# Sparse convolution on one core: uncast loads through four half-pair buffers, casts on ScalarE and GpSimd, stores on ScalarE's queue

## The chip, the core and the metric

The kernel runs on one core of a Trainium2 chip. The metric is the device time of one execution in microseconds (us). A profile's span, from the first to the last instruction, is 1.7 to 2.1 us shorter here than the time of the same execution. PE is TensorE, DVE is VectorE, ACT is ScalarE, POOL is GpSimd, SP is SyncE, which here only issues DMAs.

A run counts as fast when it is within 1.5% of the fastest run of the same kernel. Ratios are the mean time of one kernel's fast runs over that of the other's fast runs of the same rounds, so they are not quite the ratios of the medians quoted beside them. The profiled run of the kernel before (132.03 us) bears the state slow in its record, but it lies within the four runs that the first comparison rests on (131.89 to 132.76 us), so its profile stands for them.

## The reference

```python
x:      (16, 64, 64, 64) float32      # batch, channels in, h, w
weight: (128, 64, 3, 3)  float32      # 90% of it zeros
output[b, co] += weight[co, ci, kh, kw] * x_pad[b, ci, kh:kh+h, kw:kw+w]   # pad 1
```

It is a 3x3 convolution with padding. The kernel computes it densely. Two images make a pair: their 2 x 64 input channels fill the 128 partitions. There are eight pairs.

## The kernel before

A pair is worked off in four blocks of 16 rows, and blocks are numbered 0 to 31 through the whole kernel. For a block, GpSimd adds neighbouring rows into `s`, TensorE makes a shared product from `s` (6 matmuls) and two more from `x` (24 matmuls), ScalarE copies the shared product from PSUM to `pc`, and VectorE adds `pc` to the other two and writes the output tile `o`. Block 0 alone is computed directly.

```python
x_pool = tile_pool(name="x", bufs=1)             # eight bf16 tiles, one per pair
o_pool = tile_pool(name="o", bufs=7)
...
nc.sync.dma_start(out=w_sb, in_=weight...)
x_head = const_pool.tile([128, HEAD, W], FP32)   # first 36 rows of pair 0, uncast
for a, b in ((0, 9), (9, HEAD)):
    nc.sync.dma_start(out=x_head[:, a:b, :], in_=pair(0)[:, a:b, :])
nc.gpsimd.dma_start(out=xs[0][:, HEAD:H, :], in_=pair(0)[:, HEAD:H, :])   # fp32 -> bf16 in the DMA
...
for p in range(1, NP):
    nc.gpsimd.dma_start(out=xs[p], in_=pair(p))                           # fp32 -> bf16 in the DMA
...
def twos(p, o, r0):
    s = s_pool.tile([128, 8, W], BF16, name="s")                          # three buffers
    nc.gpsimd.tensor_tensor(out=s, in0=xs[p][:, r0:r0+16:2, :], in1=xs[p][:, r0+1:r0+16:2, :], op=ADD)
    shared = product([(s, G1, 0, 1)], 8)
    ...                                      # pc[n] = scalar.copy(shared[n])
    ...                                      # o[n] rows = even/odd product + pc[n], on VectorE
for p in range(NP):
    for blk in range(4): ...
    if not last:
        for n in range(2):
            nc.sync.dma_start(out=out[2 * p + n], in_=o[n])               # 2 MB each, 16 KB rows
```

The last pair is stored in two halves of 32 rows.

Of the kernel before, what the change touches and what calls it, by code (L numbers as in the profile page):

```python
# [8 lines left out]
FP32 = mybir.dt.float32  # L9
BF16 = mybir.dt.bfloat16  # L10
# [12 lines left out]
G0, G1, G2, G21, G01 = range(5)  # L23
# [4 lines left out]
def kernel(  # L28
# [6 lines left out]
    nc = tc.nc  # L35

    B, C_IN, H, W = x.shape
    C_OUT, _, KH, KW = weight.shape
    assert (B, C_IN, H, W) == (16, 64, 64, 64) and (C_OUT, KH, KW) == (128, 3, 3)
    NP = B // 2  # L40
    HEAD = 36

    const_pool = ctx.enter_context(tc.tile_pool(name="const", bufs=1))
    x_pool = ctx.enter_context(tc.tile_pool(name="x", bufs=1))
    s_pool = ctx.enter_context(tc.tile_pool(name="s", bufs=3))
    p_pool = ctx.enter_context(tc.tile_pool(name="pc", bufs=4))
    o_pool = ctx.enter_context(tc.tile_pool(name="o", bufs=7))
# [7 lines left out]
    def pair(p):  # L55
        return x[2 * p : 2 * p + 2].rearrange("n i h w -> (n i) h w")

    xs = [x_pool.tile([128, H, W], BF16, name=f"x{p}") for p in range(NP)]
    w_sb = const_pool.tile([C_OUT, C_IN * KH * KW], FP32, name="w_sb")
    nc.sync.dma_start(out=w_sb, in_=weight.rearrange("o i kh kw -> o (i kh kw)"))  # L60
    x_head = const_pool.tile([128, HEAD, W], FP32, name="x_head")
    for a, b in ((0, 9), (9, HEAD)):
        nc.sync.dma_start(out=x_head[:, a:b, :], in_=pair(0)[:, a:b, :])  # L63
    nc.gpsimd.dma_start(out=xs[0][:, HEAD:H, :], in_=pair(0)[:, HEAD:H, :])  # L64
    ident = const_pool.tile([128, 128], BF16, name="ident")
    make_identity(nc, ident)
    for p in range(1, NP):
        nc.gpsimd.dma_start(out=xs[p], in_=pair(p))  # L68


    idle_rhs = const_pool.tile([128, 128], BF16, name="idle_rhs")
# [12 lines left out]
    def tap(g, kw, n):  # L84
        return wT[64 * n : 64 * n + 64, g, (kw - n) % 3, :]

    def cast_x(copy, a, b):
        copy(out=xs[0][:, a:b, :], in_=x_head[:, a:b, :])  # L88

    def cast(g, copy, a, b):  # L90
        k = 3 * g + a % 3
        copy(out=w_bf4[:, g, a:b, :], in_=w_v[:, k : k + b - a, :])  # L92

    def transposed(g):
        wps = psum_pool.tile([128, 4, 128], FP32, name="ps")
        for j in range(3):
            src = w_bf[:, g, C_IN * j : C_IN * (j + 2)]
            nc.tensor.matmul(wps[:, j, :], src, ident, start=True, stop=True)  # L98
        return wps[:, 0:3, :]

    def difference(g, wps):
        nc.vector.tensor_tensor(out=wT[:, g], in0=wps, in1=wT[:, G1], op=SUB)  # L102
# [3 lines left out]
    cast(G0, nc.vector.tensor_copy, 0, 3)  # L106
    cast(G0, nc.vector.tensor_copy, 3, 4)
    cast(G2, nc.scalar.copy, 0, 3)
    cast(G2, nc.vector.tensor_copy, 3, 4)
    cast_x(nc.vector.tensor_copy, 0, 9)  # L110
    nc.scalar.copy(out=wT[:, G1], in_=transposed(G1))  # L111
    ps0 = transposed(G0)
    nc.vector.tensor_copy(out=wT[:, G0], in_=ps0)
    ps2 = transposed(G2)
    nc.scalar.copy(out=wT[:, G2], in_=ps2)
    cast_x(nc.scalar.copy, 9, 18)
    difference(G01, ps0)
    difference(G21, ps2)
    cast_x(nc.vector.tensor_copy, 18, HEAD)


    def product(terms, rows):
# [22 lines left out]
    def direct(p, o, r0, rows):  # L145
        ps = product(
            [(xs[p], G1, r0, 1), (xs[p], G0, r0 - 1, 1), (xs[p], G2, r0 + 1, 1)], rows
        )
        nc.scalar.copy(out=o[0][:, r0 : r0 + rows, :], in_=ps[0])  # L149
        nc.vector.tensor_copy(out=o[1][:, r0 : r0 + rows, :], in_=ps[1])  # L150

    def twos(p, o, r0):
        t0 = r0 // 2
        s = s_pool.tile([128, 8, W], BF16, name="s")
        nc.gpsimd.tensor_tensor(  # L155
            out=s, in0=xs[p][:, r0 : r0 + 16 : 2, :], in1=xs[p][:, r0 + 1 : r0 + 16 : 2, :], op=ADD
        )
        shared = product([(s, G1, 0, 1)], 8)
        pc = []
        for n in range(2):  # L160
            c = p_pool.tile([128, 8, W], FP32, name="pc")
            nc.scalar.copy(out=c, in_=shared[n])  # L162
            pc.append(c)
        even = [(xs[p], G21, r0 + 1, 2), (xs[p], G0, r0 - 1, 2)]
        odd = [(xs[p], G01, r0, 2), (xs[p], G2, r0 + 2, 2)]
        for first, terms in ((r0, even), (r0 + 1, odd)):
            ps = product(terms, 8)
            for n in range(2):
                nc.vector.tensor_tensor(  # L169
                    out=o[n][:, first : r0 + 16 : 2, :], in0=ps[n], in1=pc[n], op=ADD  # L170
                )

    for p in range(NP):
        o = [o_pool.tile([C_OUT, H, W], FP32, name="o") for _ in range(2)]
        last = p == NP - 1
        for blk in range(4):
            r0 = 16 * blk
            if BLOCKS[p][blk] == "T":
                twos(p, o, r0)
            else:  # L180
                for r, rows in ((r0, 8), (r0 + 8, 8)):
                    direct(p, o, r, rows)
            if last and blk % 2 == 1:
                for n in range(2):
                    rows = slice(r0 - 16, r0 + 16)
                    nc.sync.dma_start(out=out[2 * p + n][:, rows, :], in_=o[n][:, rows, :])
        if not last:
            for n in range(2):
                nc.sync.dma_start(out=out[2 * p + n], in_=o[n])


# [28 lines left out]
```

## Time and profile before

| kernel before | value |
|---|---|
| median time, 4 runs | 132.28 us (131.89 to 132.76) |
| span of the profiled run | 130.3 us |
| TensorE's first matmul on `x` / last matmul ends | 7.7 / 118.3 us |
| a steady block (30 matmuls) | 3.16 to 3.24 us |
| block 2 / 8 / 17 / 28 starts | 22.1 / 41.3 / 70.0 / 105.3 us |

First the page of the profile: the span in 40 equal slices (busy share of a slice in tenths; 9 is 90% or more), the DMA queues (packets, MB, time of their packets as a share of 16 engines' span), and the chain that ended last.

```profile
PE   6662499999999999999999999999999999993000
...
PEclk9985559999999999999999999999999999999655
DMA  4999999999999999999999999999599929999990
...
q1 hardware_dynamic: 3024, 35.03, 64.6%
q0 software_dynamic: 1152, 7.80, 29.1%
...
PE 79%; DMA 9%; DVE 1%; issue 1%; SPq 1%; ACT 1%; DVEq 0%
```

TensorE is full from the seventh slice (19.5 us) to its end, and it is 79% of the chain. The clock row shows half speed from about 9 to 19 us, around a gap in TensorE's work. The DMA row is full too, but for the slices near 92 and 104 us, where the engines wait for TensorE to finish a pair. So two resources are nearly exhausted at once. The second view cuts the span into stretches: first the length of the stretch, then busy us of PE, PEld (TensorE's loading of weights), DVE, ACT and POOL with instruction counts, the granted clock, DMA share and GB/s written by the DMAs (a casting load counts its bf16 bytes).

```profile
20.00:40.00 20.00, 20.00 (x190) 9.94 (x187) 15.06 (x24) 7.11 (x14) 7.61 (x7) 1.00 1.03 251
...
70.00:80.00 10.00, 10.00 (x96) 5.01 (x94) 7.82 (x14) 3.22 (x6) 3.46 (x3) 1.00 1.01 428
80.00:120.00 40.00, 38.28 (x360) 18.92 (x355) 31.36 (x51) 12.88 (x24) 10.38 (x9) 1.00 0.89 376
```

The 428 GB/s of 70 to 80 us is the pace of uncast stores alone. All 50.6 MB at 430 GB/s are 118 us.

### The profile page before, as it was taken

The numbers are of one execution on the slowest core, as the hardware profiler recorded it, in microseconds if no ns is written. First come the engines' busy times: TensorE is split into PE (matmuls) and PEld (weight loads), VectorE is DVE, ScalarE is ACT, GpSimd is POOL, SyncE is SP. The second block draws the span as 40 slices with busy tenths as digits, with TensorE's granted clock in tenths as the row PEclk, the third lists the DMA queues.
The fourth block names the chain that finished last, engine by engine and source line by source line (L and its number), as shares of the span: only waits on it lengthen the run. The fifth ranks groups of instructions, "written<-read, shape, count | busy, mean of one in ns | idle before, by whom it ended". The sixth has DMA issues, their size and how long they took to land.

```text
span 130.3 us, 2488 instructions
## 1 busy us (share of the span) xinstructions
PE 110.6 (85%) x1002; PEld 56.0 (43%) x1002; DVE 83.0 (64%) x136; ACT 38.0 (29%) x70; POOL 40.7 (31%) x45
## 2 busy tenths in 40 slices
PE   6662499999999999999999999999999999993000
PEld 6430144445444544454445445544544454440000
DVE  0350425778777868787777777777777777777000
ACT  3500313333333333333243333333333333330000
POOL 6900463333333333333333333324333330000000
PEclk9985559999999999999999999999999999999655
DMA  4999999999999999999999999999599929999990
GB/s 136 217 297 228 216 209 226 209 216 216 302 325 307 327 322 314 362 428 438 423 425 428 433 423 433 428 428 443 244 408 403 403 86 402 458 385 415 415 410 18
DMA packets 4188, 42.99 MB, mean 330 GB/s; under 512 B 464, under 2 KB 464, under 8 KB 976
## 3 DMA queue, kind: packets, MB, share of 16 engines
q1 hardware_dynamic: 3024, 35.03, 64.6%
q0 software_dynamic: 1152, 7.80, 29.1%
q8 instruction: 8, 0.13, 0.4%
q14 instruction: 4, 0.03, 0.1%
HBM read 17.07 MB, written 33.55 MB: 389 GB/s over the span
## 4 chain that ended last, share of the span: by engine, by line
PE 79%; DMA 9%; DVE 1%; issue 1%; SPq 1%; ACT 1%; DVEq 0%
PE ps L136 79%; DMA x_head<-in_x_dram 9%; DVE o L169 1%; ACT x L88 1%; DVEq L215 0%; SPq L63 0%; SPq L60 0%; DVEq L169 0%
## 5 line engine op out<-in xcount | busy, mean ns | idle before, releaser
L136 PE MATMUL ps<-x,wT 64*128 64x504 bf16 (+3 forms) x780 | 91.4, 381 | 6.7 <-ACT x L88 4.2
L169 DVE TENSOR_TENSOR o<-ps,pc 128x512 f32<-128x512 f32 x124 | 77.8, 686 | 22.4 <-PE ps L136 20.1
L136 PEld LDWEIGHTS <-wT 64*128 64x128 bf16 x966 | 52.4, 96 | 60.4 <-issue 10.4
L155 POOL TENSOR_TENSOR s<-x 128x512 bf16<-128x512 bf16 x31 | 35.6, 1152 | 65.6 <-PE ps L136 43.4
L162 ACT COPY pc<-ps 128x512 f32<-128x512 f32 x62 | 33.3, 589 | 64.3 <-issue 61.8
L136 PE MATMUL ps<-s,wT 64*128 64x512 bf16 (+1 forms) x186 | 25.8, 380 | 0.0
L88 DVE CAST x<-x_head 128x576 bf16<-128x576 f32 (+1 forms) x2 | 1.2, 611 | 7.5 <-DMA x_head<-in_x_dram 7.5
L75 PE MATMUL ps<-idle_rhs 128*128 128x128 bf16 x27 | 3.1, 313 | 1.0 <-DVE idle_rhs L72 1.0
L68 POOL DMA_DIRECT2D x<-in_x_dram x7 | 3.7, 551 | 0.0
L150 DVE COPY o<-ps 128x512 f32<-128x512 f32 x2 | 1.4, 688 | 3.4 <-PE ps L136 3.4
L75 PEld LDWEIGHTS <-idle_rhs 128*128 128x128 bf16 x27 | 2.8, 149 | 1.0 <-DVE idle_rhs L72 1.0
L88 ACT CAST x<-x_head 128x576 bf16<-128x576 f32 x1 | 0.7, 672 | 8.2 <-DMA x_head<-in_x_dram 8.2
L92 DVE CAST w_bf<-w_sb 128x192 bf16<-128x192 f32 (+1 forms) x4 | 1.2, 360 | 2.5 <-DMA w_sb<-in_weight_dram 2.5
L149 ACT COPY o<-ps 128x512 f32<-128x512 f32 x2 | 1.2, 582 | 3.6 <-PE ps L136 3.6
L92 ACT ACT_TABLE_LOAD x1 | 1.3, 1283 | 0.7 <-PEq L204 0.7
L98 PE MATMUL ps<-ident,w_bf 128*128 128x128 bf16 x9 | 1.2, 308 | 0.0
L92 ACT CAST w_bf<-w_sb 128x64 bf16<-128x64 f32 (+1 forms) x2 | 0.7, 417 | 1.4 <-DMA w_sb<-in_weight_dram 1.4
L102 DVE TENSOR_TENSOR wT<-ps,wT 128x384 bf16<-128x384 f32 x2 | 1.0, 549 | 0.0
L98 PEld LDWEIGHTS <-w_bf 128*128 128x128 bf16 x9 | 0.8, 130 | 0.4 <-DVE w_bf L92 0.4
L64 POOL DMA_DIRECT2D x<-in_x_dram x1 | 0.7, 696 | 0.8 <-POOLq L204 0.8
L72 DVE MEMSET idle_rhs<- 128x64 uint32 x1 | 0.1, 112 | 0.8 <-PEq L204 0.8
L111 ACT CAST wT<-ps 128x384 bf16<-128x384 f32 x1 | 0.5, 478 | 0.4 <-PE ps L98 0.4
(8 smaller groups left out, 1.9 us busy)
## 6 DMA issues: line engine op xcount, KB each, us to landing
out_dram<-o SPq DMA_DIRECT2D x14, 2048.0 KB, 14.4
x<-in_x_dram POOLq DMA_DIRECT2D x7, 1024.0 KB, 26.1
out_dram<-o SPq DMA_DIRECT2D x4, 1024.0 KB, 9.4
x_head<-in_x_dram SPq DMA_DIRECT2D x1, 864.0 KB, 12.3
x<-in_x_dram POOLq DMA_DIRECT2D x1, 448.0 KB, 8.8
w_sb<-in_weight_dram SPq DMA_DIRECT2D x1, 288.0 KB, 2.7
x_head<-in_x_dram SPq DMA_DIRECT2D x1, 288.0 KB, 6.0
```

The costliest lines, as they stand in the source:

```text
L68: nc.gpsimd.dma_start(out=xs[p], in_=pair(p))
L75: nc.tensor.matmul(idle_ps, idle_rhs, idle_rhs, start=True, stop=True)
L88: copy(out=xs[0][:, a:b, :], in_=x_head[:, a:b, :])
L92: copy(out=w_bf4[:, g, a:b, :], in_=w_v[:, k : k + b - a, :])
L98: nc.tensor.matmul(wps[:, j, :], src, ident, start=True, stop=True)
L102: nc.vector.tensor_tensor(out=wT[:, g], in0=wps, in1=wT[:, G1], op=SUB)
L136: nc.tensor.matmul(ps[n][:, lo:hi, c_lo:c_hi], tap(g, kw, n), src[q, a:b:step, c_lo + kw - 1 : c_hi + kw - 1], start=(i == 0), stop=(i == ...
L149: nc.scalar.copy(out=o[0][:, r0 : r0 + rows, :], in_=ps[0])
L150: nc.vector.tensor_copy(out=o[1][:, r0 : r0 + rows, :], in_=ps[1])
L155: nc.gpsimd.tensor_tensor(out=s, in0=xs[p][:, r0 : r0 + 16 : 2, :], in1=xs[p][:, r0 + 1 : r0 + 16 : 2, :], op=ADD)
L162: nc.scalar.copy(out=c, in_=shared[n])
L169: nc.vector.tensor_tensor(out=o[n][:, first : r0 + 16 : 2, :], in0=ps[n], in1=pc[n], op=ADD)
```

## The change

The intent: the loads of pair 0 no longer compete with seven casting loads, TensorE starts sooner, GpSimd generates no DMA work, and idle time of ScalarE and GpSimd is used for the casts. Each half-pair (1 MB, 8 KB per partition) lands as fp32 in one of four buffers `f`. ScalarE casts a pair's first half and GpSimd its second, at places in program order that `CAST_AFTER` lists: after block 1 pair 1, after block 3 pair 2, and so on. Loads would block stores on SP's in-order queue, so stores go to ScalarE's queue, issued a block late. The diff, cut to its core:

```diff
-    x_pool = ctx.enter_context(tc.tile_pool(name="x", bufs=1))
+    f_pool = ctx.enter_context(tc.tile_pool(name="f", bufs=4))
+    x_pool = ctx.enter_context(tc.tile_pool(name="x", bufs=4))
...
-    nc.gpsimd.dma_start(out=xs[0][:, HEAD:H, :], in_=pair(0)[:, HEAD:H, :])
-    for p in range(1, NP):
-        nc.gpsimd.dma_start(out=xs[p], in_=pair(p))
+    halves = []
+    for p in range(NP):
+        for half in range(2):
+            f = f_pool.tile([128, HALF, W], FP32, name="f")
+            cuts = (0, 9, HALF) if not halves else (0, HALF)
+            for a, b in zip(cuts, cuts[1:]):
+                r = HALF * half
+                nc.sync.dma_start(out=f[:, a:b, :], in_=pair(p)[:, r + a : r + b, :])
+            halves.append(f)
...
+    cast_x(nc.gpsimd.tensor_copy, 0, 1)
...
+    CAST_AFTER = {1: 1, 3: 2, 5: 3, 7: 4, 9: 5, 12: 6, 16: 7}
     for p in range(NP):
         for blk in range(4):
             ...                                   # the block, as before
+            store()                               # what was queued, on nc.scalar
+            q = CAST_AFTER.get(4 * p + blk)
+            if q is not None:
+                cast_x(nc.scalar.copy, q, 0)
+                cast_x(nc.gpsimd.tensor_copy, q, 1)
+            if p in (0, NP - 1): ...              # queue stores of halves
+            elif blk == 3:
+                stores += [(out[2 * p + n], o[n]) for n in range(2)]
-        if not last:
-            for n in range(2):
-                nc.sync.dma_start(out=out[2 * p + n], in_=o[n])
```

More of the change, by code (lines that the diff above doesn't have):

```diff
@@ L40 @@
     NP = B // 2
-    HEAD = 36
+    HALF = H // 2
     const_pool = ctx.enter_context(tc.tile_pool(name="const", bufs=1))
-    x_pool = ctx.enter_context(tc.tile_pool(name="x", bufs=1))
+    f_pool = ctx.enter_context(tc.tile_pool(name="f", bufs=4))
+    x_pool = ctx.enter_context(tc.tile_pool(name="x", bufs=4))
     s_pool = ctx.enter_context(tc.tile_pool(name="s", bufs=3))
@@ L56, in pair @@
         return x[2 * p : 2 * p + 2].rearrange("n i h w -> (n i) h w")
-    xs = [x_pool.tile([128, H, W], BF16, name=f"x{p}") for p in range(NP)]
     w_sb = const_pool.tile([C_OUT, C_IN * KH * KW], FP32, name="w_sb")
     nc.sync.dma_start(out=w_sb, in_=weight.rearrange("o i kh kw -> o (i kh kw)"))
-    x_head = const_pool.tile([128, HEAD, W], FP32, name="x_head")
-    for a, b in ((0, 9), (9, HEAD)):
-        nc.sync.dma_start(out=x_head[:, a:b, :], in_=pair(0)[:, a:b, :])
-    nc.gpsimd.dma_start(out=xs[0][:, HEAD:H, :], in_=pair(0)[:, HEAD:H, :])
+    halves = []
[7 more added lines that the diff above has]
+            halves.append(f)
     ident = const_pool.tile([128, 128], BF16, name="ident")
     make_identity(nc, ident)
-    for p in range(1, NP):
-        nc.gpsimd.dma_start(out=xs[p], in_=pair(p))
     idle_rhs = const_pool.tile([128, 128], BF16, name="idle_rhs")
@@ L85, in tap, with cast_x @@
         return wT[64 * n : 64 * n + 64, g, (kw - n) % 3, :]
-    def cast_x(copy, a, b):
-        copy(out=xs[0][:, a:b, :], in_=x_head[:, a:b, :])
+    xs = {}
+    def cast_x(copy, p, half, a=0, b=HALF):
+        if p not in xs:
+            xs[p] = x_pool.tile([128, H, W], BF16, name="x")
+        r = HALF * half
+        copy(out=xs[p][:, r + a : r + b, :], in_=halves[2 * p + half][:, a:b, :])
     def cast(g, copy, a, b):
@@ L108 @@
     cast(G2, nc.scalar.copy, 0, 3)
-    cast(G2, nc.vector.tensor_copy, 3, 4)
-    cast_x(nc.vector.tensor_copy, 0, 9)
+    cast(G2, nc.gpsimd.tensor_copy, 3, 4)
+    cast_x(nc.vector.tensor_copy, 0, 0, 0, 9)
     nc.scalar.copy(out=wT[:, G1], in_=transposed(G1))
@@ L115 @@
     nc.scalar.copy(out=wT[:, G2], in_=ps2)
-    cast_x(nc.scalar.copy, 9, 18)
+    cast_x(nc.scalar.copy, 0, 0, 9, 18)
     difference(G01, ps0)
     difference(G21, ps2)
-    cast_x(nc.vector.tensor_copy, 18, HEAD)
+    cast_x(nc.vector.tensor_copy, 0, 0, 18, HALF)
+    cast_x(nc.gpsimd.tensor_copy, 0, 1)
     def product(terms, rows):
@@ L171, in twos, with store @@
                 )
+    CAST_AFTER = {1: 1, 3: 2, 5: 3, 7: 4, 9: 5, 12: 6, 16: 7}
+    stores = []
+    def store():
+        for dst, src in stores:
+            nc.scalar.dma_start(out=dst, in_=src)
+        stores.clear()
     for p in range(NP):
         o = [o_pool.tile([C_OUT, H, W], FP32, name="o") for _ in range(2)]
-        last = p == NP - 1
         for blk in range(4):
@@ L182 @@
                     direct(p, o, r, rows)
-            if last and blk % 2 == 1:
-                for n in range(2):
+            store()
[3 more added lines that the diff above has]
+                cast_x(nc.gpsimd.tensor_copy, q, 1)
+            if p in (0, NP - 1):
+                if blk % 2 == 1:
                     rows = slice(r0 - 16, r0 + 16)
-                    nc.sync.dma_start(out=out[2 * p + n][:, rows, :], in_=o[n][:, rows, :])
-        if not last:
-            for n in range(2):
-                nc.sync.dma_start(out=out[2 * p + n], in_=o[n])
+                    stores += [(out[2 * p + n][:, rows, :], o[n][:, rows, :]) for n in range(2)]
+            elif blk == 3:
+                stores += [(out[2 * p + n], o[n]) for n in range(2)]
+    store()
 _INS = ['x', 'weight']
```

## The prediction

> **What bounds it now.** The chain of waits is 79% TensorE (one run from 14.7 to 117.1 us), after a 12.3 us load of the second piece of `x_head`; a store tail ends it (span 130.3). The windows show PE busy without a gap from 20 to 117 us; a block of 30 matmuls takes 3.24 us in the timeline. DMA is nearly as full: mean share 1.0 from 3 to 91 us. Uncast queue: 35.03 MB in 64.6% of 16 engines' span, 416 GB/s; casting queue: 15.6 MB read in 29.1%, 411 GB/s. So a casting load costs by its fp32 bytes, and loading uncast saves no DMA time. All 50.6 MB at the 430 GB/s of the 70-90 us windows take 118 us; with 1.6 us of start and 3.2 us of end, no version of this can span under about 123 us. DMA idles near 92 and 104-107 us, waiting for PE.
>
> **What the change removes.** The early loads' sharing with seven casting loads. `x_head` rows 9-36 took 12.3 us for 0.86 MB; in order on one queue the first half-pair should land near 6 us. PE then starts near 5 us instead of 7.7, loses the 4.2 us gap before 14.7, and most of the half-clock stretch of 10 to 19 us.
>
> **What it adds.** ScalarE: seven casts of 128x2048. From 672 ns for 576 elements and 305 for 64, about 1.9 us each, 13 us; plus 18 store issues at about 0.45 us. It was 29% busy. GpSimd: eight casts, 1.8 to 3.3 us each (estimate; the Trainium skill, "GPSIMD Engine Reference", Performance versus the Vector engine, gives 1.03 to 1.8 cycles per element at 1.2 GHz; this trace has no such cast), ahead of `s` adds, in order.
>
> **What gives the gain back.** Half h waits until half h-4 is cast, and casts stand in order among blocks. Until block 9 the schedule casts a pair every two blocks (6.5 us), while its load and two blocks' stores are 4.2 MB, 9.8 us of DMA. Blocks 1 and 2 start near 11.8 and 17 us (18.5 and 22.1 before, 5 us ahead), but half 9 (pair 4) shares the engines with pair 0's stores, lands near 36 us, and GpSimd's cast and add hold block 8 until about 39.5 us (41.5 before). An idle PE of 3 us may also fall to half clock again (the Trainium skill, "TensorE: Matmul & The Clock Gate", Part 1: window about 3.4 us; here 0.50 after the 10.5-14.7 gap). So 1 to 3 us of the 5 remain. Then come 20 blocks at 3.24 us. The last 20 us are its stores and pair 7's, DMA-paced, and start about 1 us later, because ScalarE issues them after the next block's evictions.
>
> **Prediction.** Span about 129.3, time 131.2 us (132.42 before), 127.5 to 134.8. Faster by over 2%: 0.33; within 2%: 0.53; slower: 0.14.
>
> **What would show it.** First real matmul near 5 us; block 2 near 17 us; a PE gap of 2-5 us between 30 and 45 us, whose waits lead over `s` on GpSimd to a `f` load; DMA time in sum unchanged (94% of 130 us); ScalarE near 53 us busy; DMA idle of some us after 80 us again; about 13 us from PE's end.
>
> **What would make it wrong.** Loads that get more than half the engines beside stores: no gap, 126-127 us. A GpSimd cast over 3.5 us, or loads that get only a third against 16 KB store rows: gaps at several casts, over 135. ScalarE blocked by a cast's load, delaying `pc`.

## The result, and the profile after

The changed kernel took 141.51 us in the median of 4 runs (140.92 to 142.19) against 132.28 us. The ratio of the fast runs is 1.070 (95% interval 1.064 to 1.076): 7% slower, and outside the stated range.

The same parts of the page, for the changed kernel:

```profile
PE   7794859997941999983999999999999999995000
...
PEclk9999999999998699997799999999999999999955
DMA  5899999999996999999999999298939957899991
...
q10 hardware_dynamic: 2880, 33.56, 56.9%
q1 hardware_dynamic: 2592, 17.07, 32.2%
...
PE 40%; DMA 26%; issue 14%; POOL 8%; SPq 1%; ACT 1%; DVE 1%; DVEq 0%; POOLq 0%
```

TensorE now has holes, at about 12 and 18 us, near 42, and near 63 us. Both of the later ones are followed by a stretch at half clock. Only 40% of the chain is TensorE; 26% is waiting for the landing of `f`. DMA time in sum is hardly changed: (56.9 + 32.2)% of 139.9 us are 124.7 us, against (64.6 + 29.1)% of 130.3 us, 122.1 us. The stretches show where the time went:

```profile
0.00:20.00 20.00, 14.18 (x108) 8.17 (x110) 7.50 (x15) 7.70 (x11) 7.54 (x12) 1.00 0.87 329
20.00:40.00 20.00, 18.96 (x178) 9.94 (x175) 13.58 (x22) 11.32 (x15) 8.78 (x7) 1.00 1.00 397
40.00:50.00 10.00, 5.16 (x38) 2.37 (x37) 3.06 (x6) 1.59 (x3) 5.17 (x4) 0.83 0.88 327
...
60.00:70.00 10.00, 7.33 (x56) 3.33 (x54) 4.34 (x8) 4.00 (x5) 6.31 (x5) 0.83 1.00 428
...
80.00:120.00 40.00, 40.00 (x378) 21.41 (x376) 30.99 (x50) 13.97 (x27) 15.66 (x14) 1.00 0.79 334
```

TensorE loses 4.8 of the 10 us from 40 to 50 us and 2.7 us from 60 to 70 us. From 80 us on it is as full as before, and the DMA share falls to 0.79, because the stores now wait for TensorE. The table of waits (engine and what it was about to do, what it waited for: us in sum, times, longest):

```profile
POOL x L96 <- DMA f<-in_x_dram: 40.8, 7, 8.3
DVE o L178 <- PE ps L145: 36.4, 27, 6.9
...
PE ps L145 <- POOL s L164: 12.8, 6, 4.8
```

TensorE waited 12.8 us in six pieces for `s` from GpSimd, and GpSimd waited 40.8 us in seven pieces for loads of `f`. These two rows belong together, as the timeline around the longest hole shows (start us, duration, engine, line, operation, output<-input, count, and in brackets the idle time before it and what ended it):

```profile
41.89 1.89 POOL L96 CAST x<-f 128x2048 bf16<-128x2048 f32 x1 [7.32 <-DMA f<-in_x_dram]
43.74 2.25 POOL L164 TENSOR_TENSOR s<-x 128x512 bf16<-128x512 bf16 x2
...
44.94 1.46 PE L145 MATMUL ps<-s,wT 64*128 64x512 bf16 x6 [4.84 <-POOL s L164]
```

GpSimd stood 7.32 us at its cast of pair 4's second half, whose load landed at 41.84 us. Only then could it make `s` for block 8, and TensorE had stood still for 4.84 us. But block 8 belongs to pair 2, whose data had long been there. Pair 4 is not needed before block 16. This is head-of-line blocking: work that is needed now waits on an in-order engine behind work that isn't.

| | before | changed | difference |
|---|---|---|---|
| block 2 starts | 22.06 | 19.50 | -2.6 us |
| block 8 starts | 41.27 | 44.94 | +3.7 us |
| block 17 starts | 70.04 | 79.71 | +9.7 us |
| block 28 starts | 105.30 | 114.96 | +9.7 us |
| span | 130.3 | 139.9 | +9.6 us |

So the kernel did gain at the start, lost 6.2 us by block 8 and another 6.0 us by block 17, and ran in step with the kernel before from there to the end. Of the 6.0 us after block 8, the half-clock stretches take part: blocks 8 and 13 took 4.48 and 4.73 us in place of 3.24.

### The profile page after: what moved, and what is told of

Same layout as the page of the kernel before. It is cut to its first block, busy times and chain, and to the rows that moved or that the text cites. A ratio compares the mean times of both kernels' runs of the same rounds, so it can differ in the third digit from the quotient of the medians.

```text
span 139.9 us, 2527 instructions
## 1 busy us (share of the span) xinstructions
PE 113.4 (81%) x1002; PEld 59.2 (42%) x1002; DVE 82.8 (59%) x135; ACT 50.9 (36%) x77; POOL 51.0 (36%) x46
## 3 DMA queue, kind: packets, MB, share of 16 engines
q10 hardware_dynamic: 2880, 33.56, 56.9%
q1 hardware_dynamic: 2592, 17.07, 32.2%
## 4 chain that ended last, share of the span: by engine, by line
PE 40%; DMA 26%; issue 14%; POOL 8%; SPq 1%; ACT 1%; DVE 1%; DVEq 0%; POOLq 0%
PE ps L145 40%; DMA f<-in_x_dram 26%; POOL s L164 6%; POOL x L96 2%; ACT x L96 1%; SPq L68 1%; DVE o L178 1%; DVEq L237 0%; SPq L60 0%; POOLq L164 0%; POOLq L96 0%; DVEq L178 0%
## 5 line engine op out<-in xcount | busy, mean ns | idle before, releaser
L145 PE MATMUL ps<-x,wT 64*128 64x504 bf16 (+3 forms) x780 | 92.4, 384 | 0.8 <-DVE x L96 0.8
L145 PEld LDWEIGHTS <-wT 64*128 64x128 bf16 x966 | 55.6, 97 | 66.9 <-issue 21.0
L145 PE MATMUL ps<-s,wT 64*128 64x512 bf16 (+1 forms) x186 | 26.9, 392 | 12.8 <-POOL s L164 12.8
L96 POOL CAST x<-f 128x2048 bf16<-128x2048 f32 x8 | 15.1, 1890 | 41.9 <-DMA f<-in_x_dram 40.8
L96 ACT CAST x<-f 128x2048 bf16<-128x2048 f32 (+1 forms) x8 | 14.0, 1754 | 3.3 <-DMA f<-in_x_dram 3.2
L96 DVE CAST x<-f 128x576 bf16<-128x576 f32 (+1 forms) x2 | 1.1, 543 | 2.6 <-DMA f<-in_x_dram 2.6
```

The costliest lines, as they stand in the source:

```text
L96: copy(out=xs[p][:, r + a : r + b, :], in_=halves[2 * p + half][:, a:b, :])
L145: nc.tensor.matmul(ps[n][:, lo:hi, c_lo:c_hi], tap(g, kw, n), src[q, a:b:step, c_lo + kw - 1 : c_hi + kw - 1], start=(i == 0), stop=(i == ...
```

## The experiments

Theory A: the casts stand too early in the program for the pace at which loads land, and block what stands behind them. Rivals: B, the uncast loads cost DMA capacity; C, stores on ScalarE's queue hold up its evictions; D, ScalarE's casts do the harm rather than GpSimd's; A1, a refinement, says why loads land late: engines are shared packet for packet, which favours the larger rows.

| run | median us | before, same chip | ratio of fast runs |
|---|---|---|---|
| changed kernel, first chip | 141.51 | 132.28 | 1.070 |
| e1 late casts | 130.81 | 130.76 | 1.018 (1.008 to 1.027) |
| e2 stores in 8 KB rows | 138.72 | 130.76 | 1.075 (1.059 to 1.092) |
| e3 four named buffers | 138.34 | 130.76 | 1.072 (1.056 to 1.088) |
| e4 before, with the stores of the change | 131.16 | 130.76 | 1.020 (1.009 to 1.032) |
| e8 changed kernel again | 140.68 | 130.99 | 1.071 (1.065 to 1.078) |
| e5 GpSimd's casts late | 136.98 | 130.99 | none |
| e6 ScalarE's casts late | 155.90 | 130.99 | none |
| e7 e2 and e3 together | 138.18 | 130.99 | 1.053 (1.047 to 1.058) |
| e12 late casts again | 130.85 | 132.16 | none |
| e9 before, half stores | 129.74 | 132.16 | none |
| e10 late casts, six buffers | 129.25 | 132.16 | none |
| e11 late casts, loads of pairs | 128.54 | 132.16 | none |

The ratios of e1 to e4 need care. On that chip the kernel before spread from 128.40 to 133.17 us in seven runs, and the rule for fast runs keeps only its quickest ones, so its mean there lies below its median of 130.76; by the record all four verdicts are unclear. On the last chip the same happened: ten of its eleven runs lie between 130.58 and 132.79 us and one at 128.11, which leaves too few fast runs for a ratio. For small differences the medians and the traces are the better evidence, and no verdict is claimed for e9 to e12. What makes the kernel before vary was not found.

### e1: all casts late

```diff
-    CAST_AFTER = {1: 1, 3: 2, 5: 3, 7: 4, 9: 5, 12: 6, 16: 7}
+    CAST_AFTER = {2: 1, 6: 2, 10: 3, 14: 4, 18: 5, 22: 6, 26: 7}
```

> Only the places of the casts move: pair q is cast after block 4q-2, two blocks before its first use, in place of up to nine blocks before. Theory A (head-of-line blocking: GpSimd stands at a cast whose load has not landed, while the s sum that the next block needs waits behind it, although the cast's own pair is needed only many blocks later): the TensorE gaps before blocks 6, 8, 13 and 17 (1.0, 4.8, 2.7 and 0.2 us in the changed kernel) vanish, block 2 starts near 18 us, every later block takes 3.24 us, span near 127 us, time near 129 us, below the kernel before. Rival B (DMA capacity: the uncast loads themselves cost more engine time, or the loads come too late for their data's own use): the gaps move to the first block of a pair, and the time stays over 138 us.

Measured: 130.81 us (130.28 to 131.39), span 128.4 us. From the page of this run:

```profile
PE   6954799999999999999999999999999999970000
...
DMA  4999999999999999999999999999999999999980
...
q10 hardware_dynamic: 2880, 33.56, 62.3%
q1 hardware_dynamic: 2592, 17.07, 33.5%
```

After block 2, which started at 18.6 us, every block took its steady time, and TensorE ended at 114.8 us, 3.5 us earlier than in the kernel before. One line of seven numbers undoes the whole loss of 10 us. The load and store sizes, the queues, the engines and the amount of casting are those of the changed kernel, so theory A holds, and rival B falls as the cause of the loss. (One hole stayed in e1: 2.73 us before block 1, where `s` stands behind GpSimd's cast of pair 0's second half.) The time is 1.8 us above the expected 129 and only equals that of the kernel before by medians; against that kernel's quickest runs it is 1.8% slower. The DMA row suggests why: it is full from the second slice to the last but one. The two queues' times add to (62.3 + 33.5)% of 128.4 us, 123 us, and the tail after TensorE's end grew from 12.0 to 13.6 us. So the limit appears to have moved from TensorE to the DMA engines.

### e2: stores in rows of 8 KB

```diff
-                stores += [(out[2 * p + n], o[n]) for n in range(2)]
+                stores += [(out[2*p+n][:, a:a+HALF, :], o[n][:, a:a+HALF, :]) for n in range(2) for a in (0, HALF)]
```

> The whole-pair stores are issued at the same place, but each as two DMAs of 32 rows, so that a store's packets are 8 KB like a load's instead of 16 KB. Theory A1 (queues share an engine packet for packet, so against 16 KB rows an 8 KB load gets a third): the share of the load queue rises from about a third to a half in the windows after 50 us, the load that block 13's sum stands behind lands near 55 us instead of 61.9, the gaps before blocks 13 and 17 and the half-clock stretch after them vanish, the gap of 4.8 us before block 8 stays (pair 0's stores were 8 KB already); time near 137 us. Rival (the share is set by bytes, or by who issued first): no change in the shares, time 141 us.

Measured: 138.72 us (137.13 to 139.18), 2.0 us under the changed kernel's median of the later run e8, which was on another chip. The DMA view gives, per queue, packets, MB and share of the 16 engines' time in a window in which both queues have work. The changed kernel, 52 to 74 us (q10 stores, q1 loads):

```profile
q10 hardware_dynamic: 431, 6.31, 67.3%
q1 hardware_dynamic: 419, 3.05, 33.1%
```

With stores in 8 KB rows, 51 to 67 us:

```profile
q1 hardware_dynamic: 461, 3.33, 50.7%
q10 hardware_dynamic: 449, 3.31, 49.1%
```

And the kernel before, 36 to 52 us (q0 casting loads, q1 stores):

```profile
q0 software_dynamic: 226, 1.71, 51.2%
q1 hardware_dynamic: 223, 3.39, 50.5%
```

In all three the packet counts of the queues are nearly equal, and the bytes follow the row size. An 8 KB load beside a 16 KB store gets 3.05 of 9.4 MB, a third. Equal rows give equal bytes; the casting loads of the kernel before read 16 KB per packet and so had half of the engines' time. So A1's sharing holds in these windows. The load that block 13 stood behind landed at 59.0 us in place of 61.9 (60.4 in e8), short of the expected 55, and block 13 followed block 12 by 3.38 us in place of 6.01. Part of this is that block 12 itself started 1.3 us later than in the changed kernel. The gap before block 8 stayed, as expected, and the block after it ran at half clock (5.4 us), which the expected 137 us had left out. The Trainium skill, "DMA: Bandwidth & Descriptors", Queues, rings and completion order, says that an engine goes round-robin between the queues that have work, a packet at a time; these counts agree with it. (The page's packet is typically 9 to 17 descriptors, while a packet of this profile is one row, so the counts show equal turns, not how long a turn is.)

### e3: four named buffers

```diff
-    f_pool = ctx.enter_context(tc.tile_pool(name="f", bufs=4))
+    f_pool = ctx.enter_context(tc.tile_pool(name="f", bufs=1))
-            f = f_pool.tile([128, HALF, W], FP32, name="f")
+            f = f_pool.tile([128, HALF, W], FP32, name=f"f{len(halves) % 4}")
```

> Four named buffers in place of a pool of four: load h then waits for load h-4's cast, as the prediction took for granted; in the changed kernel the compiled order lets the tenth half wait for the eighth's cast by GpSimd, and it is issued at 32.4 us. If that wait counts: the tenth half is issued near 27 us, lands near 39.5 instead of 41.8, block 8 starts 2 us earlier, time near 139 us. If not (the stores only take the turn): time within 1 us of 141.5.

Measured: 138.34 us (137.33 to 139.83), 2.3 us under e8's median, on another chip. The tenth half was issued at 26.1 us in place of 32.4, but it landed at 40.8 us. The changed kernel's two profiles have 41.8 (first chip) and 39.6 us (e8), so nothing was gained there, and block 8 started at 43.9 us, between their 44.9 and 42.7. The buffer order was a real wait, but a harmless one for this landing: the engines had other transfers to move. In both kernels they had moved 15.2 MB when the tenth half landed, 11.0 MB on the load queue and 4.1 MB of pair 0's stores. What the named buffers did change is later. The load that block 13 stood behind landed at 56.8 us in place of 61.9 (60.4 in e8), and the hole before block 13 was gone. The stores kept their 16 KB rows here, so the buffer order alone can also close this hole. So the time is near the expected 139 us, but not for the expected reason.

### e4: the kernel before with the change's stores

The loads of the kernel before, and the `stores`, `store()` and half stores of pair 0 as in the diff of the change.

> The kernel before with the change's stores alone: on ScalarE's queue, issued a block later, pair 0 in halves; loads as before. Theory A (the loss lies in loads and casts): within 1 us of the kernel before, 132 to 133.3 us. Rival C (stores in ScalarE's program order hold up the evictions): over 135 us.

Measured: 131.16 us (130.74 to 132.22) against a median of 130.76 us of the kernel before. Its blocks started within 0.3 us of those of the kernel before from block 2 on (block 28 at 105.56 against 105.30 us), and the spans are 130.4 and 130.3 us. The time lies below the expected 132 to 133.3 us, which was drawn around the first chip's 132.28 us. Rival C falls: the stores on ScalarE's queue cost nothing that can be seen here, nor in e1, which keeps them too.

### e8: the changed kernel again

> The changed kernel unaltered, on the chip of these runs, so that the others have a partner of the same chip. Expected 140 to 142 us, block 8 starting near 45 us and block 17 near 79 us as in its first profile.

Measured: 140.68 us (140.36 to 142.68), block 8 at 42.7 us and block 17 at 78.3 us. The time is as expected; block 8 came 2 us earlier than in the first profile, and the next block took 5.6 us at half clock, which gave 2.4 us back.

### e5 and e6: one engine's casts late

```diff
             if q is not None:
                 cast_x(nc.scalar.copy, q, 0)
+            q = LATE.get(4 * p + blk)              # {2: 1, 6: 2, 10: 3, ...}, as in e1
+            if q is not None:
                 cast_x(nc.gpsimd.tensor_copy, q, 1)
```

e6 is the mirror image, with ScalarE's casts late and GpSimd's early.

> Only GpSimd's casts move to the late places (after block 4q-2); ScalarE's stay at the early ones. If it is the sums on GpSimd that stand behind casts (theory A), TensorE's gaps before blocks 6, 8, 13 and 17 go from 8.7 us in sum to under 3, and the time to 129 to 134 us. If ScalarE's casts, standing before the evictions, cost as much (rival D), gaps of several us stay and the time is over 137.

> The mirror of it: only ScalarE's casts move late, GpSimd's stay early. Theory A: the gap before block 8 stays 5 us or grows, since buffers come free later; time 140 us or more. Rival D: time under 135.

Measured: e5 took 136.98 us (133.61 to 138.37) and e6 155.90 us (151.32 to 157.02). Neither has enough fast runs for a ratio, since their runs spread too far; the profiled ones are not of the fast kind. In e5 the holes before blocks 6 and 8 were gone (block 8 at 36.5 us), as theory A says, but the time missed the expected range, because a hole of another kind came at 58.7 us:

```profile
60.66 1.90 ACT L96 CAST x<-f 128x2048 bf16<-128x2048 f32 x1 [7.44 <-DMA f<-in_x_dram]
62.47 2.04 ACT L171 COPY pc<-ps 128x512 f32<-128x512 f32 x4
...
63.10 5.40 PE L145 MATMUL ps<-x,wT 64*128 64x512 bf16 x24 [4.43 <-ACT pc L171]
```

ScalarE stood 7.44 us at a cast whose load had not landed; the evictions `pc` waited behind it, and TensorE waited 4.43 us. So rival D is partly right: either engine blocks in the same way. (e5's quickest run, 133.61 us, lies inside theory A's range; it was not profiled.) e6 is worse than the changed kernel: its twelfth half landed at 54.9 us in place of 48.8, which fits buffers that come free later because their casts come later, and GpSimd's early casts then stand longer for their loads. Only when both engines' casts came late (e1) did all holes after block 1 close.

### e7: both repairs of the load pace, casts early

> Both repairs of the load rate together (four named buffers, stores in 8 KB rows), the early casts unchanged. If the late landing is all that counts, the gap before block 8 (5.6 and 6.0 us over the steady step with either repair alone) falls under 2 us and the time to 132-134. If the position of the casts is what counts, the tenth half still lands after 38 us, block 8 starts after 42 us, and the time stays at 136 to 139, though the gaps from block 13 on are gone.

Measured: 138.18 us (137.81 to 138.35), ratio 1.053. The decisive spot in its timeline:

```profile
41.16 1.89 POOL L96 CAST x<-f 128x2048 bf16<-128x2048 f32 x1 [7.52 <-DMA f<-in_x_dram]
43.01 2.25 POOL L164 TENSOR_TENSOR s<-x 128x512 bf16<-128x512 bf16 x2
44.20 1.47 PE L145 MATMUL ps<-s,wT 64*128 64x512 bf16 x6 [5.04 <-POOL s L164]
...
45.44 4.85 PE L145 MATMUL ps<-x,wT 64*128 64x512 bf16 x24
```

With equal shares and the buffers in order, the tenth half still landed only at 41.1 us, TensorE still stood for 5.04 us, and the next block ran at half clock. From block 13 on there was no hole. This is the second outcome: better loads repair the later holes, and the first one needs the cast moved. e1, without these repairs, took 130.81 us on another chip, about 7 us less. Neither both repairs with late casts nor early casts with the sum `s` put ahead of them were run, so 7 us is no exact price of the cast's place.

### e12, e9, e10, e11: what remains

e12 is e1 with more rounds. e9 is the kernel before with every pair stored in halves (`if blk % 2 == 1` for all pairs). e10 is e1 with `f` at 6 buffers and `o` at 6. e11 is e1 with whole-pair loads, 16 KB rows, three buffers of a pair, and `o` at 6.

> The late casts once more, with more rounds, because the first chip's runs of the kernel before spread from 128.4 to 133.2 us. Expected 130 to 131.5 us, within 1% of the kernel before: TensorE ends some 3.5 us earlier than before, but the DMA engines are busy from start to end and set the time.

> The kernel before, with every pair stored in two halves of 32 rows as soon as each is done (only the last pair was). If the DMA idle time near 92 and 104 us, waiting for whole pairs, lies on the path of its tail: the idle time goes, the tail after TensorE's end shrinks from 12 to about 9 us, span near 127, time 2 to 2.5% below the kernel before. If the DMA floor is higher than worked out: under 1% gained.

> Late casts with six half-pair buffers (and six output tiles in place of seven, to make room). Loads run further ahead, so the load queue runs dry less often, and its packets in a dry queue took 330 to 430 ns for 8 KB in place of 309. If that is what keeps the late casts above the floor: 1 us less than the late casts, 129 to 130. If not: the same within 0.7 us.

> Late casts, with loads of whole pairs (16 KB rows, three buffers, six output tiles). Packet-for-packet sharing predicts that loads now get half of the engines beside 16 KB stores, as the casting loads of the kernel before did; TensorE has no gaps in either case, so the time stays within 1 us of the late casts, 129 to 131.

Measured: e12 130.85 us (130.38 to 132.14), e9 129.74 (128.66 to 131.11), e10 129.25 (128.88 to 130.98), e11 128.54 (127.95 to 129.30), the kernel before 132.16 (128.11 to 132.79). By medians e11 is 2.7% quicker than the kernel before and about 9% quicker than the changed kernel on its chips (141.51 and 140.68 us); ten of eleven runs of the kernel before were slower than all six of e11. But its one run that counts as fast, 128.11 us, lies within e11's range, so by fast runs it is not shown that e11 beats the kernel before. In e11 the loads had half of the engines beside the stores, as A1 says (50 to 57 us):

```profile
q1 hardware_dynamic: 92, 1.51, 50.5%
q10 hardware_dynamic: 99, 1.51, 50.4%
```

Its span was 126.4 us, and its queues' times add to (62.7 + 33.1)% of it, 121 us. e11 came out 0.5 us below its expected range. e9 gained 1.8% by medians, a little less than expected: on the page of its profiled run, which was not a fast one, the DMA holes near 92 and 104 us are gone, with some idle time left in the last tenth, and a tail of 11.0 us, not 9. e10 gained 1.6 us on e12, as expected if dry queues cost time. That dry queues (load queues with little left to move) are the cause was not isolated: e10 changed the number of output tiles too.

## Why the prediction was wrong

- **Bounds.** TensorE at 3.24 us per block and a DMA floor near 123 us of span: not contradicted. The profiles of e1, e10 and e11 came to 128.4, 127.6 and 126.4 us, with DMA full; no run's span went under 126 us. That 123 us itself is the floor was not shown.
- **Uncast loads save no DMA time.** Right: 124.7 us of packet time against 122.1 us.
- **The start.** Too hopeful. "in order on one queue the first half-pair should land near 6 us": it landed at 8.93 us, the first matmul on `x` started at 6.03 instead of 5 us, and block 2 at 19.50 instead of 17. The windows show 329 GB/s in the first 20 us, not 430. (e8, the same kernel, has 8.03, 5.24 and 18.59 us, so a part of the miss varies from run to run.) The blocking that the prediction foresaw for block 8 was at work here too: block 1's `s` stood behind GpSimd's cast of pair 0's second half, which landed at 11.44 us and was cast until 13.39, so block 1 started at 14.55 us instead of 11.8.
- **Costs of casts and issues.** Right, with some luck: 1.91 us on ScalarE and 1.89 us on GpSimd, 0.46 us per store issue, and ScalarE was busy 50.9 us (53 predicted). A straight line through the two durations that the text quotes gives 1.73 us for ScalarE's cast, not 1.9; the 1.8 cycles per element that it quotes give 3.1 us on GpSimd, not 3.3; and the stores are 20, not 18. None of it mattered.
- **The mechanism, and the step that failed.** The mechanism was right, and named in the text: GpSimd's cast and add hold block 8, by a wait that leads from `s` to an `f` load. A size was off. The step that failed is "lands near 36 us, and GpSimd's cast and add hold block 8 until about 39.5 us". The load landed at 41.84 us and block 8 started at 44.94, 5.4 us later than predicted. One premise was plainly false, "Half h waits until half h-4 is cast": in the compiled program the tenth half waited for GpSimd's cast of the eighth, and it was issued at 32.38 us, just after that cast ended at 32.35. But e3 made the premise true and the half landed at 40.8 us, between the two profiles of the changed kernel (41.8 and 39.6). What was mis-sized is the pace of the DMA engines: 329 and 397 GB/s in the first and second 20 us, in place of the 430 GB/s of the calculation, are 2.7 MB less, 6.2 us at 430 GB/s, of which the 1.6 us before the first transfer were in the prediction. The 15.2 MB that had been moved at 41.84 us would take 35.4 us at 430 GB/s, 37.0 with the 1.6 us of start, close to the predicted 36. In the trace the 2304-byte rows at the start took 122 ns each on average, 19 GB/s per engine, against mostly 309 ns for 8 KB, 26.5 GB/s; and from 22 to 24 us, with no other queue at work, 8 KB packets took 430 ns on average. Why they did so was not isolated.
- **After block 8.** "So 1 to 3 us of the 5 remain. Then come 20 blocks at 3.24 us" failed as well. From block 8 to block 28 it took 70.0 us instead of 64.8, 5.2 us more: the hole before block 13, and half-clock stretches after both holes. The text had this case among what would make it wrong ("loads that get only a third against 16 KB store rows: gaps at several casts, over 135") but gave it no weight in the sum, although the row sizes were in the diff. The unequal rows had a part in the hole before block 13, since e2 closed it with equal rows; but e3 closed it too, with the 16 KB rows kept and the buffers in order, so they were not its only cause. It was not the whole story either: e7 had no such hole and was still 5.3% slower than the kernel before. The two misses, 5.4 us up to block 8 and 5.2 us after it, make up the whole difference between the predicted span of 129.3 us and the measured 139.9.
- **The tail.** About right: 12.0 us (13 predicted) from TensorE's end to the end of the span, and the DMA engines idle again after 80 us (share 0.79).

The larger error was one of judgement. Having seen that the cast of pair 4 stood in front of block 8, eight blocks before its use, the prediction took that as a small delay to be computed from a load's landing time. With a landing time uncertain by 6 us, everything behind that cast was uncertain by 6 us, and each slip also cost a stretch at half clock.

## What to carry to other kernels

On an in-order engine, put an instruction that waits for a load just ahead of its first use, not as soon as a buffer might be filled: the work behind it pays for every microsecond that the load is late. When two queues share the DMA engines, compare their row sizes before dividing the bandwidth, since in these traces the queues moved equal numbers of packets, one row each, and the larger rows won. And when a kernel has two resources near their limit, a change that relieves one is worth at most the distance to the other: here 3.5 us of TensorE time gained in e1 did not show in the median, most likely because the DMA engines, full to the end, had become the limit.

## What the Trainium skill lacked or had wrong

- "DMA: Bandwidth & Descriptors", Queues, rings and completion order: it has the round-robin by packet, but not that bytes then follow the row size, where a packet of the profile is one row. The runs show 3.05 MB of 8 KB loads beside 6.31 MB of 16 KB stores with 419 and 431 packets.
- "DMA: Bandwidth & Descriptors", Specifications: its row of about 358 GB/s for HBM per core, read alone, misleads for a kernel on one core. Here the stores alone ran at 428 GB/s for 10 us, and e11 moved 401 GB/s, read and written, over its whole span. The same page's section Bandwidth does have 425 GB/s for one core while the other core of its pair is idle, which agrees, so the row only lacks that remark.
- "TensorE: Matmul & The Clock Gate", Part 1: it gives one idle window of about 3.4 us as the condition for half clock, and says that the window is free-running. The traces agree with a free-running window, since within each trace the granted clock changes only at whole multiples of 3.41 us from its first change, but not with the need for a wholly idle one. Cut all 14 traces into windows on that grid. Of those that began at full clock, all 26 in which TensorE was idle for 2.16 us or more were followed by half clock; of 51 with 0.3 to 1.93 us idle none was. (The ends of matmuls are modelled, so these figures are approximate.) So the place of a hole on the grid matters as well as its length: the hole of 2.73 us before block 1 put 2.18 us into one window in e1, and half clock followed; in e12 the same hole was split into 1.64 and 1.09 us, and none did. In the changed kernel the hole of 2.67 us before block 13 was followed by half clock, that of 2.55 us before block 1 was not.
- "GPSIMD Engine Reference", Performance versus the Vector engine: no figure for a cast. Here fp32 to bf16 of 128x2048 took 1.89 us, 0.92 ns per element, at the low end of what its range for simple loops gives.
